# Two matmuls in place of three in the up projection of a two-layer decoder trunk

## The chip, the cores and the metric

The kernel runs on one core of one Trainium2 chip. The metric is the device time of one execution in microseconds (us), taken by the hardware. Engine names: PE is TensorE (PEld its weight loads), DVE is VectorE, ACT is ScalarE, POOL is GpSimd, SP is SyncE, which issues the weight transfers.

## What is computed

The reference is a trunk of two layers on 256 positions of width 1024, all in float32. Each layer has a mixer (attention in three branches, gated) and then a two-step feed-forward part, which is what the change touches:

```
x = x + y @ w_out
hm = rms_norm(x, g_mlp)
x = x + jnp.square(jax.nn.relu(hm @ w_up)) @ w_down      # w_up 1024 x 4096, w_down 4096 x 1024
```

## The kernel before

**Precision.** PE multiplies operands rounded to a shorter float (type fp32r). To come near float32 each operand is split in two: `hi`, the rounded value, which ACT writes, and `lo`, the rest, which DVE writes. A product then takes three matmuls, hi by hi, hi by lo, lo by hi, all accumulated in one PSUM bank; `mm3` (L144 to L147) issues them. In its calls the first argument pair is the stationary operand (loaded by a weight load) and the second the moving one.

**Groups.** The whole program is a list of groups, in an order written by hand. A unit is one weight transfer of up to 1 MB into one of three `raw` buffers; a group is a part of a unit, whose weights are split to `whi` and `wlo` (five buffers each) by `split_to`, L136 on ACT and L137 on DVE. The loop at the end of the kernel goes through the groups: it emits the matmuls of group j, then the split of group j+3 (`LOOK = 3`), then the transfers of the units after it, then deferred work, then the evacuation of group j. Every engine runs its own instructions strictly in that order.

**The feed-forward part of a layer.** `feat_half(l, "mlp", n)` transposes the residual stream and writes the activations as `mlpT`: two tile pairs (`ahi`, `alo`), each 128 x 4 x 256, with four of the eight slices of the 1024 features; they begin 4 elements behind a boundary of 64 elements (`FWD`), where those of the mixer begin on it. `up_first` computes the first 512 columns of the up projection, four tiles of 128 columns with one PSUM bank each; `up_unit(c)` computes 256 columns, two tiles that share one bank, in the second of its two groups. For each tile and each of the eight feature slices `mm3` runs with 128 x 128 weights as stationary operand and 256 positions as moving one. `up_evac(c, p)` (L687 to L701) evacuates them: ACT takes the relu out of PSUM (L695, or L693 twice where the tiles have a bank each), ACT squares it into `uh` (L698), DVE squares it into `sq` (L699), and DVE subtracts `uh` from it to give `ul` (L700). `down_unit(c, n)` multiplies `uh`, `ul` of two `up_unit`s by 512 columns of `w_down`, 24 matmuls of 512 columns, into four banks that stay open through the layer (`dacc`). The order is `up_first`, `up_unit(2)`, and then for c from 0 to 7: `down_unit(c, 0)`, `up_unit(2c+3)`, `down_unit(c, 1)`, `up_unit(2c+4)`. In layer 0 the key and value projections of the memory for layer 1 stand behind `down_unit(4, 1)`.

**PSUM.** `ps()` takes the bank that has been free longest out of eight, `pf()` gives it back.

Of the kernel before, what the change touches and what calls it, by code (L numbers as in the profile page):

```python
# [40 lines left out]
def hybrid_kernel(ctx, tc, x, mem, memT, gains, g_final, rope, masks, w_in, w_pa, w_pb, w_pm,  # L41
# [20 lines left out]
    def sb(shape, dt, tag, bufs, shift=None):  # L62

        n = int(np.prod(shape[1:]))
        if n * (2 if dt == BF16 else 4) % (4 * LINE):
            return small.tile(shape, dt, tag=tag, name=tag, bufs=bufs)
        if shift is None:  # L70
            return pool.tile(shape, dt, tag=tag, name=tag, bufs=bufs)
        t = pool.tile([shape[0], n + LINE], dt, tag=tag, name=tag, bufs=bufs)[:, shift:shift + n]
        return t if len(shape) == 2 else t.rearrange("p (a b) -> p a b", a=shape[1])

    LINE, FWD = 64, 4
    BACK = LINE - FWD
# [65 lines left out]
    def mm3(o, lh, ll, rh, rl, start, stop):  # L144
        nc.tensor.matmul(o, lhsT=lh, rhs=rh, start=start, stop=False)  # L145
        nc.tensor.matmul(o, lhsT=lh, rhs=rl, start=False, stop=False)  # L146
        nc.tensor.matmul(o, lhsT=ll, rhs=rh, start=False, stop=stop)  # L147


# [85 lines left out]
    def qk_unit(l, col, kind, key0, rope_it, act, wsrc, ntile, rows_key):  # L235
        st = {}

        def emit(first, last, ks):
            def f(hi, lo):
# [3 lines left out]
                for i in range(ntile):  # L243
                    for c, k in enumerate(ks):
                        ah, al = tiles[k // 4]
                        mm3(st["p"][i][:, :S], hi[:, c, i * P:(i + 1) * P],
                            lo[:, c, i * P:(i + 1) * P], ah[:, k % 4, :], al[:, k % 4, :],
                            k == 0, k == KT - 1)
# [30 lines left out]
    def v_unit(l, col, n, act, wsrc, key, rows):  # L279
# [3 lines left out]
        def emit(first, last, ks):  # L283
            def f(hi, lo):
# [3 lines left out]
                for t in range(2):  # L288
                    for c, k in enumerate(ks):
                        ah, al = tiles[k // 4]  # L290
                        tt = slice(t * P, (t + 1) * P)
# [180 lines left out]
    def layer(l):  # L472
# [10 lines left out]
        for n in range(2):  # L483
            for br in range(3):
# [3 lines left out]
                def emit(first, last, ks, br=br, n=n, b=b):  # L488
                    def f(hi, lo):
                        if first:  # L490
                            b["p"] = [ps() for _ in range(2)]
                        for t in range(2):
                            tt = slice(t * P, (t + 1) * P)
                            for c, k in enumerate(ks):
                                ah, al = st["hT"][k // 4]
                                mm3(b["p"][t], ah[:, k % 4, tt], al[:, k % 4, tt], hi[:, c, :],
                                    lo[:, c, :], k == 0, k == KT - 1)
# [72 lines left out]
        for n in range(2):  # L570
# [59 lines left out]
            def y_transpose(n=n):  # L630
                for t in range(2):
# [4 lines left out]
                    if t == 0:  # L636
                        st["yT", n] = (sb([P, 4, S], F32R, "ahi", 2, 0),
                                       sb([P, 4, S], F32R, "alo", 2, 0))
                    hi, lo = st["yT", n]
                    tt = slice(t * P, (t + 1) * P)  # L640
# [7 lines left out]
        for half in range(2):  # L648
            for n in range(2):
                def emit(first, last, ks, half=half, n=n):  # L650
                    def f(hi, lo):
# [3 lines left out]
                        for t in range(2):  # L655
                            tt = slice(t * P, (t + 1) * P)
                            for c, k in enumerate(ks):
                                ah, al = st["yT", k // 4]
                                mm3(acc[t, n], ah[:, k % 4, tt], al[:, k % 4, tt], hi[:, c, :],
# [26 lines left out]
        def up_evac(c, p):  # L686
# [3 lines left out]
            ul = sb([P, 2, S], F32R, "qk", 11, 0)  # L690
            if len(p) == 2:
                for i in range(2):
                    nc.scalar.activation(tt[:, i, :], p[i][:, :S], AF.Relu)  # L693
            else:
                nc.scalar.activation(tt.rearrange("p a t -> p (a t)"), p[0], AF.Relu)  # L695
            for t in p:
                pf(t)
            nc.scalar.activation(uh, tt, AF.Square)  # L698
            nc.vector.tensor_tensor(sq, tt, tt, op=ALU.mult)  # L699
            nc.vector.tensor_sub(ul, sq, f32(uh))  # L700
            us[c] = (uh, ul)  # L701

        def up_first():
            b = {}

            def emit(ks):
                def f(hi, lo):
                    if ks[0] == 0:
                        b["p"] = [ps() for _ in range(4)]
                    for i in range(4):  # L710
                        for cc, k in enumerate(ks):
                            ah, al = st["mlpT"][k // 4]
                            mm3(b["p"][i][:, :S], hi[:, cc, i * P:(i + 1) * P],
                                lo[:, cc, i * P:(i + 1) * P], ah[:, k % 4, :], al[:, k % 4, :],
                                k == 0, k == KT - 1)
                    if ks[-1] == KT - 1:
# [10 lines left out]
        def up_unit(c):  # L727
            b = {}

            def emit(last):  # L730
                def f(hi, lo):
                    if not last:
                        b["w"] = (hi, lo)
                        return None
                    p = ps()
                    for i in range(2):
                        for (wh, wl), k0 in ((b["w"], 0), ((hi, lo), 4)):
                            ah, al = st["mlpT"][k0 // 4]
                            for cc in range(4):
                                mm3(p[:, i * S:(i + 1) * S], wh[:, cc, i * P:(i + 1) * P],  # L740
                                    wl[:, cc, i * P:(i + 1) * P], ah[:, cc, :], al[:, cc, :],
                                    k0 + cc == 0, k0 + cc == KT - 1)
                    return lambda: up_evac(c, [p])
                return f
# [114 lines left out]
    def feat_half(l, what, n):  # L859
# [4 lines left out]
        if n == 0:  # L864
            L[ll][dst] = []
        shift = FWD if what == "mlp" else 0
        hi = sb([P, 4, S], F32R, "ahi", 2, shift)
        lo = sb([P, 4, S], F32R, "alo", 2, shift)
        L[ll][dst].append((hi, lo))
        for kp in range(2):  # L870
# [121 lines left out]
    def w_load(k, c):  # L992
# [20 lines left out]

    L[0]["hT"] = [(sb([P, 4, S], F32R, "ahi", 2, 0), sb([P, 4, S], F32R, "alo", 2, 0))
                  for _ in range(2)]

# [8 lines left out]
    def first_operand(k):  # L1025
        hi, lo = L[0]["hT"][k // 4]
        p = first_ps[k // 2]
# [127 lines left out]
```

## Time and profile before

| | before |
|---|---|
| device time, median of 3 runs | 776.96 us (775.22 to 777.06) |
| the profiled execution: device time | 775.68 us |
| its span, first to last instruction | 773.9 us |
| mean granted TensorE clock | 0.998 |
| PE busy | 759.4 us, 4749 matmuls |
| DVE busy | 545.1 us |
| ACT busy | 463.4 us |
| read from HBM | 137.52 MB |

The busy time of PE counts the whole life of a matmul, and matmuls overlap: a stream of them is read by the distance from one start to the next. Idle time of an engine costs nothing unless PE waits for it.

### The profile page before, as it was taken

What the parts mean: (1) busy time and instruction counts of PE and PEld (TensorE: products, weight loads), DVE (VectorE), ACT (ScalarE), POOL (GpSimd) and SP (SyncE); (2) the same over time, 40 slices, a digit from 0 to 9 for tenths busy, and PEclk for the clock granted to TensorE, in tenths of its full rate; (3) what the DMA queues carried; (4) which work ended last, traced back from release to release, by engine and by line L of the source; (5) the groups of instructions that cost most, each with busy time, mean ns of one, the idle gap of its engine ahead of it and who ended that gap; (6) DMA issues with size and microseconds to landing.
All of it is one profiled execution on the core that took longest, in us unless ns stands there. A gap on an engine that the chain in (4) does not pass through costs nothing.

```text
span 773.9 us, 12157 instructions
## 1 busy us (share of the span) xinstructions
PE 759.4 (98%) x4749; PEld 687.7 (89%) x4749; DVE 545.1 (70%) x905; ACT 463.4 (60%) x784; POOL 73.9 (10%) x79
## 2 busy tenths in 40 slices
PE   8999999999999999999999999999999999999996
PEld 6998899888899989998989899988889998999895
DVE  4899999759674655666468899987787656545554
ACT  5687878883573454565455877868546535444542
POOL 1333030003000000000004221200110000000000
PEclk9999999999999999999999999999999999999999
DMA  8847454544656547645536454443565564566431
GB/s 282 278 146 242 153 166 137 186 136 164 218 164 218 194 154 251 217 164 176 192 123 215 157 186 151 164 163 136 191 207 164 174 217 165 165 216 230 161 127 54
DMA packets 92201, 139.35 MB, mean 180 GB/s; under 512 B 2928, under 2 KB 53104, under 8 KB 92144
## 3 DMA queue, kind: packets, MB, share of 16 engines
q1 hardware_dynamic: 92000, 138.55, 54.2%
q8 instruction: 37, 0.61, 0.3%
q14 instruction: 20, 0.16, 0.1%
q10 hardware_dynamic: 144, 0.02, 0.0%
HBM read 137.52 MB, written 1.05 MB: 179 GB/s over the span
## 4 chain that ended last, share of the span: by engine, by line
PE 57%; issue 30%; DVE 7%; ACT 4%; POOL 2%; DMA 1%; POOLq 0%; ACTq 0%; DVEq 0%
PE ps_b L146 17%; PE ps_b L145 17%; PE ps_b L147 17%; DVE wlo L137 2%; PE ps_b L412 1%; ACT whi L136 1%; DVE qk L206 1%; PE ps_b L439 1%; POOL rs L225 1%; POOL rc L226 1%; PE ps_b L332 1%; PE ps_b L331 1%; PE ps_b L438 1%; DMA raw<-in_w_mkv 1%; PE ps_b L1041 0%
## 5 line engine op out<-in xcount | busy, mean ns | idle before, releaser
L137 DVE TENSOR_TENSOR wlo<-raw,whi 128x1024 fp32r<-128x1024 f32 (+2 forms) x266 | 307.8, 1180 | 62.9 <-ACT whi L136 58.5
L136 ACT ACTIVATE whi<-raw 128x1024 fp32r<-128x1024 f32 (+2 forms) x266 | 260.4, 1008 | 54.7 <-PE ps_b L147 41.2
L145 PE MATMUL ps_b<-ahi,whi 128*128 128x256 f32 x736 | 207.2, 282 | 0.0
L147 PE MATMUL ps_b<-ahi,wlo 128*128 128x256 f32 x736 | 206.1, 280 | 0.0
L146 PE MATMUL ps_b<-alo,whi 128*128 128x256 f32 x736 | 206.0, 280 | 0.0
L146 PEld LDWEIGHTS ps_b<-alo,whi 128*128 128x128 f32 x736 | 138.1, 188 | 1.2
L145 PEld LDWEIGHTS ps_b<-ahi,whi 128*128 128x128 f32 x736 | 138.1, 188 | 1.2
L147 PEld LDWEIGHTS ps_b<-ahi,wlo 128*128 128x128 f32 x736 | 138.0, 188 | 0.0
L145 PE MATMUL ps_b<-whi,ahi 128*128 128x512 f32 (+1 forms) x320 | 125.1, 391 | 1.8 <-ACT whi L136 1.8
L146 PE MATMUL ps_b<-wlo,ahi 128*128 128x512 f32 (+1 forms) x320 | 121.5, 380 | 0.5 <-DVE wlo L137 0.5
L147 PE MATMUL ps_b<-whi,alo 128*128 128x512 f32 (+1 forms) x320 | 121.5, 380 | 0.0
L147 PE MATMUL ps_b<-whi,qk 128*128 128x512 f32 x256 | 100.2, 391 | 0.0
L146 PE MATMUL ps_b<-wlo,qk 128*128 128x512 f32 x256 | 100.1, 391 | 0.0
L145 PE MATMUL ps_b<-whi,qk 128*128 128x512 f32 x256 | 99.8, 390 | 0.0
L699 DVE TENSOR_TENSOR P<-P 128x512 f32<-128x512 f32 x32 | 22.1, 692 | 106.7 <-ACT P L695 103.7
L695 ACT ACTIVATE P<-ps_b 128x512 f32<-128x512 f32 x28 | 16.7, 597 | 121.9 <-PE ps_b L147 121.9
L145 PEld LDWEIGHTS ps_b<-whi,ahi 128*128 128x128 f32 x320 | 60.2, 188 | 11.1 <-ACT whi L136 2.6
L147 PEld LDWEIGHTS ps_b<-whi,alo 128*128 128x128 f32 x320 | 60.1, 188 | 10.3
L146 PEld LDWEIGHTS ps_b<-wlo,ahi 128*128 128x128 f32 x320 | 60.3, 188 | 9.6 <-DVE wlo L137 1.1
L147 PEld LDWEIGHTS ps_b<-whi,qk 128*128 128x128 f32 x256 | 48.0, 188 | 10.2
L146 PEld LDWEIGHTS ps_b<-wlo,qk 128*128 128x128 f32 x256 | 48.1, 188 | 9.4
L145 PEld LDWEIGHTS ps_b<-whi,qk 128*128 128x128 f32 x256 | 48.1, 188 | 9.3
(146 smaller groups left out, 882.4 us busy)
## 6 DMA issues: line engine op xcount, KB each, us to landing
raw<-in_w_up SPq DMA_DIRECT2D x32, 1024.0 KB, 5.7
raw<-in_w_down SPq DMA_DIRECT2D x32, 1024.0 KB, 5.0
raw<-in_w_in SPq DMA_DIRECT2D x24, 1024.0 KB, 5.1
raw<-in_w_in SPq DMA_DIRECT2D x24, 768.0 KB, 4.6
raw<-in_w_out SPq DMA_DIRECT2D x8, 1024.0 KB, 5.0
raw<-in_w_mkv SPq DMA_DIRECT2D x4, 1024.0 KB, 5.3
raw<-in_w_pm SPq DMA_DIRECT2D x4, 512.0 KB, 3.3
raw<-in_w_pb SPq DMA_DIRECT2D x4, 512.0 KB, 3.5
```

Source lines behind the costliest of these rows:

```text
L136: nc.scalar.activation(hi, src, AF.Copy)
L137: nc.vector.tensor_sub(lo, src, f32(hi))
L145: nc.tensor.matmul(o, lhsT=lh, rhs=rh, start=start, stop=False)
L146: nc.tensor.matmul(o, lhsT=lh, rhs=rl, start=False, stop=False)
L147: nc.tensor.matmul(o, lhsT=ll, rhs=rh, start=False, stop=stop)
L206: nc.vector.tensor_sub(q[b, j, :], qf[a, :], f32(q[a, j, :]))
L225: nc.gpsimd.tensor_tensor(sh, sh, sinr, op=ALU.mult)
L226: nc.gpsimd.tensor_tensor(c, c, sh, op=ALU.add)
L331: nc.tensor.matmul(p[:, o:o + n], lhsT=qt, rhs=ka[:, j, :n], start=True, stop=False)
L332: nc.tensor.matmul(p[:, o:o + n], lhsT=qt, rhs=kb[:, j, :n], start=False, stop=True)
L695: nc.scalar.activation(tt.rearrange("p a t -> p (a t)"), p[0], AF.Relu)
L699: nc.vector.tensor_tensor(sq, tt, tt, op=ALU.mult)
```

## The change

The activations become one tile `ax` of 128 x 2 x 4 x 256 with both halves in it, `operand(shift)`, so that one access pattern can take the hi and the lo half of a feature slice, 2 x 256 columns 1024 elements apart. It replaces the pairs `ahi`, `alo` everywhere, also in the mixer, which still reads them as two halves. For `mlpT` it begins 8 elements behind the boundary (`HALF`), not 4. In the up projection `mm2` takes the place of `mm3`: one matmul of 512 columns, the hi weights by both halves, and one of 256, the lo weights by the hi half, into the first 256 columns. The product of the hi weights with the lo half stands in the last 256 columns of the bank, and `up_evac` adds it. Each tile of `up_unit` now has a bank of its own.

```diff
+    def mm2(o, lh, ll, rr, start, stop):
+        nc.tensor.matmul(o, lhsT=lh, rhs=rr, start=start, stop=False)
+        nc.tensor.matmul(o[:, :S], lhsT=ll, rhs=rr[:, 0, :], start=False, stop=stop)
+
+    def operand(shift=0):
+        t = sb([P, 2, 4, S], F32R, "ax", 2, shift)
+        return t[:, 0], t[:, 1], t
...
-            if len(p) == 2:
-                for i in range(2):
-                    nc.scalar.activation(tt[:, i, :], p[i][:, :S], AF.Relu)
-            else:
-                nc.scalar.activation(tt.rearrange("p a t -> p (a t)"), p[0], AF.Relu)
-            for t in p:
-                pf(t)
-            nc.scalar.activation(uh, tt, AF.Square)
-            nc.vector.tensor_tensor(sq, tt, tt, op=ALU.mult)
+            for i in range(2):
+                nc.scalar.activation(tt[:, i, :], p[i][:, S:], AF.Copy)
+            for i in range(2):
+                nc.vector.tensor_tensor(tt[:, i, :], p[i][:, :S], tt[:, i, :], op=ALU.add)
+                pf(p[i])
+            nc.vector.scalar_tensor_tensor(sq, tt, 0.0, tt, op0=ALU.max, op1=ALU.mult)
+            nc.scalar.activation(uh, sq, AF.Copy)
             nc.vector.tensor_sub(ul, sq, f32(uh))
...
-                            ah, al = st["mlpT"][k // 4]
-                            mm3(b["p"][i][:, :S], hi[:, cc, i * P:(i + 1) * P],
-                                lo[:, cc, i * P:(i + 1) * P], ah[:, k % 4, :], al[:, k % 4, :],
-                                k == 0, k == KT - 1)
+                            mm2(b["p"][i], hi[:, cc, i * P:(i + 1) * P],
+                                lo[:, cc, i * P:(i + 1) * P],
+                                st["mlpT"][k // 4][2][:, :, k % 4, :], k == 0, k == KT - 1)
...
-                    p = ps()
+                    p = [ps() for _ in range(2)]
                     for i in range(2):
                         for (wh, wl), k0 in ((b["w"], 0), ((hi, lo), 4)):
-                            ah, al = st["mlpT"][k0 // 4]
                             for cc in range(4):
-                                mm3(p[:, i * S:(i + 1) * S], wh[:, cc, i * P:(i + 1) * P],
-                                    wl[:, cc, i * P:(i + 1) * P], ah[:, cc, :], al[:, cc, :],
+                                mm2(p[i], wh[:, cc, i * P:(i + 1) * P],
+                                    wl[:, cc, i * P:(i + 1) * P],
+                                    st["mlpT"][k0 // 4][2][:, :, cc, :],
                                     k0 + cc == 0, k0 + cc == KT - 1)
-                    return lambda: up_evac(c, [p])
+                    return lambda: up_evac(c, p)
...
-        shift = FWD if what == "mlp" else 0
-        hi = sb([P, 4, S], F32R, "ahi", 2, shift)
-        lo = sb([P, 4, S], F32R, "alo", 2, shift)
-        L[ll][dst].append((hi, lo))
+        hi, lo, both = operand(HALF if what == "mlp" else 0)
+        L[ll][dst].append((hi, lo, both))
```

## Rows read from the trace of the kernel before

**Rows 1.** The profile page: busy time by engine, and granted clock by slice.

```profile
PE 759.4 (98%) x4749; PEld 687.7 (89%) x4749; DVE 545.1 (70%) x905; ACT 463.4 (60%) x784; POOL 73.9 (10%) x79
PEclk9999999999999999999999999999999999999999
```

**Rows 2.** Busy time by stretch, steady feed-forward parts of layers 0 and 1.

```profile
core 0: us, PE busy (x) PEld busy (x) DVE busy (x) ACT busy (x) POOL busy (x), PEclk, DMA share, GB/s
239.15:384.50 145.35, 145.35 (x963) 133.53 (x962) 84.38 (x92) 73.38 (x95) 0.00 (x0) 1.00 0.59 194
615.00:750.00 135.00, 135.00 (x873) 123.26 (x872) 73.17 (x72) 61.65 (x72) 0.00 (x0) 1.00 0.56 186
```

**Rows 3.** Timeline of PE: starts (first column) at the edges of an up unit.

```profile
233.26 0.28 PE L145 MATMUL ps_b<-ahi,whi 128*128 128x256 f32 x1
233.38 0.28 PE L146 MATMUL ps_b<-alo,whi 128*128 128x256 f32 x1
233.50 0.28 PE L147 MATMUL ps_b<-ahi,wlo 128*128 128x256 f32 x1
...
238.95 0.39 PE L145 MATMUL ps_b<-whi,qk 128*128 128x512 f32 x1
239.19 0.40 PE L146 MATMUL ps_b<-wlo,qk 128*128 128x512 f32 x1
```

**Rows 4.** Timeline of PE: the last 60 matmuls of 512 columns.

```profile
752.92 0.39 PE L147 MATMUL ps_b<-whi,qk 128*128 128x512 f32 x1
...
766.30 0.39 PE L146 MATMUL ps_b<-wlo,qk 128*128 128x512 f32 x1
```

**Rows 5.** Timeline of PE: 256 columns elsewhere, memory keys, then queries and keys.

```profile
341.34 0.28 PE L146 MATMUL ps_b<-wlo,gate 128*128 128x256 f32 x1
...
343.50 0.28 PE L147 MATMUL ps_b<-whi,gate 128*128 128x256 f32 x1
...
413.14 0.28 PE L146 MATMUL ps_b<-alo,whi 128*128 128x256 f32 x1
...
417.93 0.28 PE L147 MATMUL ps_b<-ahi,wlo 128*128 128x256 f32 x1
```

**Rows 6.** Timeline of ACT, DVE and SP around one evacuation.

```profile
261.51 0.60 ACT L695 ACTIVATE P<-ps_b 128x512 f32<-128x512 f32 x1 [4.64 <-PE ps_b L147]
262.14 0.64 ACT L698 ACTIVATE qk<-P 128x512 fp32r<-128x512 f32 x1
262.68 2.94 ACT L136 ACTIVATE whi<-raw 128x1024 fp32r<-128x1024 f32 x3
...
262.14 0.69 DVE L699 TENSOR_TENSOR P<-P 128x512 f32<-128x512 f32 x1 [4.01 <-ACT P L695]
262.94 0.69 DVE L700 TENSOR_TENSOR qk<-P,qk 128x512 fp32r<-128x512 f32 x1
263.76 3.49 DVE L137 TENSOR_TENSOR wlo<-raw,whi 128x1024 fp32r<-128x1024 f32 x3
...
265.01 0.37 SPq L121 DMA_DIRECT2D raw<-in_w_down  x1
```

**Rows 7.** Timeline of PE: starts of the next two units behind that evacuation.

```profile
261.31 0.39 PE L145 MATMUL ps_b<-whi,qk 128*128 128x512 f32 x1
...
266.80 0.28 PE L145 MATMUL ps_b<-ahi,whi 128*128 128x256 f32 x1
...
268.22 0.28 PE L145 MATMUL ps_b<-ahi,whi 128*128 128x256 f32 x1
```

**Rows 8.** Groups of instructions by form: the nearest kin of the new evacuation.

```profile
L223 DVE TENSOR_TENSOR rc<-cosr,ps_b 128x256 f32<-128x256 f32 x24 | 10.0, 415 | 0.1
L851 DVE SCALAR_TENSOR_TENSOR x<-ps_b,r,x 128x512 f32<-128x512 f32 x7 | 5.2, 749 | 7.7 <-PE ps_b L147 7.7
L693 ACT ACTIVATE P<-ps_b 128x256 f32<-128x256 f32 x8 | 3.0, 379 | 5.7 <-PE ps_b L147 5.5
```

**Rows 9.** Who waited for whom: total us, times, longest.

```profile
ACT P L695 <- PE ps_b L147: 121.9, 28, 4.6
```

**Rows 10.** The profile page, transfers: KB each, median us from issue to landing.

```profile
raw<-in_w_down SPq DMA_DIRECT2D x32, 1024.0 KB, 5.0
```

More of the change, by code (lines that the diff above doesn't have):

```diff
@@ L72, in sb @@
         t = pool.tile([shape[0], n + LINE], dt, tag=tag, name=tag, bufs=bufs)[:, shift:shift + n]
-        return t if len(shape) == 2 else t.rearrange("p (a b) -> p a b", a=shape[1])
-    LINE, FWD = 64, 4
+        names = "abc"[:len(shape) - 1]
+        return t.rearrange(f"p ({' '.join(names)}) -> p {' '.join(names)}",
+                           **dict(zip(names[1:], shape[2:])))
+    LINE, FWD, HALF = 64, 4, 8
     BACK = LINE - FWD
@@ L244, in f @@
                     for c, k in enumerate(ks):
-                        ah, al = tiles[k // 4]
+                        ah, al = tiles[k // 4][:2]
                         mm3(st["p"][i][:, :S], hi[:, c, i * P:(i + 1) * P],
@@ L289, in f @@
                     for c, k in enumerate(ks):
-                        ah, al = tiles[k // 4]
+                        ah, al = tiles[k // 4][:2]
                         tt = slice(t * P, (t + 1) * P)
@@ L494, in f @@
                             for c, k in enumerate(ks):
-                                ah, al = st["hT"][k // 4]
+                                ah, al, _ = st["hT"][k // 4]
                                 mm3(b["p"][t], ah[:, k % 4, tt], al[:, k % 4, tt], hi[:, c, :],
@@ L636, in y_transpose @@
                     if t == 0:
-                        st["yT", n] = (sb([P, 4, S], F32R, "ahi", 2, 0),
-                                       sb([P, 4, S], F32R, "alo", 2, 0))
-                    hi, lo = st["yT", n]
+                        st["yT", n] = operand()
+                    hi, lo, _ = st["yT", n]
                     tt = slice(t * P, (t + 1) * P)
@@ L657, in f @@
                             for c, k in enumerate(ks):
-                                ah, al = st["yT", k // 4]
+                                ah, al, _ = st["yT", k // 4]
                                 mm3(acc[t, n], ah[:, k % 4, tt], al[:, k % 4, tt], hi[:, c, :],
@@ L1011, in hybrid_kernel @@
     nc.sync.dma_start(mask, masks)
-    L[0]["hT"] = [(sb([P, 4, S], F32R, "ahi", 2, 0), sb([P, 4, S], F32R, "alo", 2, 0))
-                  for _ in range(2)]
+    L[0]["hT"] = [operand() for _ in range(2)]
     first_ps = {}
@@ L1025, in first_operand @@
     def first_operand(k):
-        hi, lo = L[0]["hT"][k // 4]
+        hi, lo, _ = L[0]["hT"][k // 4]
         p = first_ps[k // 2]
```

## The prediction

> **What bounds the kernel now.** I read the page first. PE is busy 98% of the span, and every slice shows a granted clock of nine tenths or more [rows 1]; the stretch views give 1.00, the 2.4 GHz level [rows 2]. So neither a cold clock nor a slow stage is to be mended. The same stretch view, over the steady feed-forward parts of both layers, is the one that matters, because all that is changed lies there: PE is busy for the whole of 145.35 and 135.00 us, while DVE works 58 and 54% of them, ACT 50 and 46%, and the DMA engines 59 and 56%. A busy PE is no proof of a full one, so I went on to the timeline of PE, and read distances from start to start. One up unit runs from 233.26 to 238.95 [rows 3]: 48 matmuls of 256 columns in 5.69 us, 118.5 ns each, with no gap inside. The last 60 matmuls of 512 columns start 13.38 us apart, first to last [rows 4]: 59 steps of 226.8 ns. Twice 118.5 is 237.0, so 512 columns in two matmuls cost 10.2 ns more than in one. This is all that the change can win: it streams just as many columns as before, 768 for each tile and slice. The waits say why nothing else wins: in 28 evacuations ACT sat idle 121.9 us in all until PE was done [rows 9], so ACT and DVE wait for PE and not PE for them.
>
> **PE: the sum.** `up_first` has 4 tiles by 8 slices, 32 sets of three matmuls; each of the 14 `up_unit`s has 2 by 8, 16 sets. That is 256 sets a layer and 512 in all. A set costs 3 x 118.5 = 355.5 ns now. It becomes one matmul of 512 columns and one of 256. At the paces of rows 3 and 4 these are 226.8 + 118.5 = 345.3 ns, 10.2 ns less; 512 times that is 5.2 us. One weight load in three goes too, 512 of 4749, but loads run beside matmuls and I give nothing for it on its own.
>
> Both paces are borrowed. For the 256 columns the trace has a faster stretch, the memory keys: 19 steps in 2.16 us, 113.7 ns; and a slower one, queries and keys of layer 1: 40 steps in 4.79 us, 119.8 ns [rows 5]. Same width, same three-way pattern, other operands and other offsets in their tiles; so up to 6 ns hang on where operands lie, and the change moves `mlpT` from 4 elements behind the boundary to 8. For the 512 columns the faster end is 226.8 (no stretch is lower); the slower end is the first step of a down unit, 238.95 to 239.19, 240 ns as rounded [rows 3]. A set thus lies between 226.8 + 113.7 = 340.5 and 240 + 119.8 = 359.8 ns, which is 7.7 us won to 2.2 us lost. I take 345.3, since the up unit's own pace is the nearest row for 256 columns, and the long even run for 512 is nearer to an unbroken stream than the first step behind another unit.
>
> The trace shows no moving operand in two pieces: every one is a single run of 256 or 512 columns. Below, a break between pieces costs nothing (the columns are streamed either way, so I exclude a gain); above, as much as the boundary of two matmuls, 10.2 ns, which would eat the win. I take nothing, as the end that adds no instruction, and keep the other as a rival.
>
> A rule of the Trainium skill speaks against the change: "TensorE: Matmul & The Clock Gate", section "Wait — 56ns, not 53.3ns?", puts the fixed cost of a matmul in a warm stream at about 2.5 ns over its columns. As an estimate by that page, 512 matmuls fewer would give only 1.3 us. The trace does not agree: rows 3 and 4 differ by 10.2 ns a matmul; but part of that may belong to something other than the number of matmuls, and then the rule's small figure would be nearer.
>
> **The evacuation: added work, hidden.** Now ACT takes 0.60 us (L695) and 0.64 (L698), DVE 0.69 twice (L699, L700) [rows 6]. After: ACT copies two halves of 256 columns at 0.379 each, like L693, and makes `uh` as before, 1.40 in all against 1.24; DVE adds two halves at 0.415, like L223, takes relu and square in one instruction of 512, at least 0.69 like L699 and at most 0.749 like L851, and subtracts in 0.69: 2.21 to 2.27 against 1.38 [rows 6, 8]. Over 32 evacuations that is 5 us of ACT and 28 us of DVE; both have some 40% of these stretches free [rows 2], so the busy time alone costs nothing.
>
> What counts is the chain, since each engine is in order. `uh` now waits for DVE, and ACT's next weight split waits behind it. Today: the unit ends at 261.31 [rows 7], the relu starts at 261.51, the next `wlo` split at 263.76 and is done at 265.01, where SP issues the transfer that waited for its buffer [rows 6]. After: the first tile is complete half a unit earlier, so its copy and sum are done. The second tile's copy runs 261.5 to 261.9, its sum to 262.3, relu and square to 263.1, `uh` to 263.75; then `whi` (2.94 / 3, about 1.0) to 264.75 and `wlo` (3.49 / 3, about 1.2) to 266.0, 1.0 us later than now. This split belongs to the second group of the next up unit. That unit starts at 266.80 and first needs it after 12 matmuls, at 268.22 [rows 7]; with faster units 0.2 earlier, 268.0. So the slack falls from 3.2 to 2.0 us and PE does not wait. Behind `up_first` two evacuations stand in a row, some 2 us more work in the chain; the same count leaves about 1.2 us there. Cover gone would show at once: every microsecond that the split is late beyond this would stop PE in each of 28 up units.
>
> The queue behind: SP's transfer is issued 1.0 us later, at 266.0. At 5.0 us to landing [rows 10] its data are there at 271.0. They are split behind the next up unit's evacuation; two periods lie between 238.95 and 261.31 [rows 3, 7], so one is 11.18 us and that is from 263.76 + 11.2 = 274.9 on. Hidden by 4 us. Two banks for each `up_unit` in place of one: four are held by `dacc`, four are left, so two units alternate, and a bank is used again a whole unit of `down` later. The tile `ax` joins two tiles that were always taken and released together; in the mixer nothing is issued more or less. There the offsets of operands beyond the boundary of 64 change; I take no change, with 6 ns on some 670 matmuls of 256 columns of queries and keys, 4 us, as the bound in both directions [rows 5].
>
> **Sum.** 5.2 us off. The profiled execution took 775.68 us (span 773.9, 1.8 around it), so 770.5. The median of the runs shown is 776.96, which gives 771.8. The two differ by more than I can place; I put the time between them, 771.1.
>
> **Rivals.**
> - *A larger win.* The lo weights are now loaded behind 512 columns and not 256, and the hi ones of the next set behind 256 as now. If the excess of 118.5 over 113.7 comes from loads that barely fit behind 256 columns, the set falls to 340.5 ns: 7.7 us, 768.6 us. For it: 113.7 exists. Against: the memory keys have the same loads behind the same columns and run at it already, so it may be only where operands lie. Chance 0.18.
> - *Nothing to speak of.* The break in the moving operand costs what a boundary of two matmuls costs, 10.2 ns, or only a small part of 10.2 belongs to the number of matmuls, as the page has it: 0 to 1.3 us, 775.0 to 776.3. For it: no row with a broken operand. Against: both plain paces are even over dozens of steps. Chance 0.12.
> - *Slower.* The two-piece operand is read worse than a boundary: 512 columns at the 240 ns of the first step behind another unit, plus a break of 10.2, with 256 at 119.8: 370.0 ns a set, 14.5 more, 7.4 us, 783.7. It decides from 345.3 + 10.2 on: each ns beyond costs 0.5 us. Against it: the 240 stands only in the first steps of a unit. Chance 0.06. The late split is part of no sum: it needs 2.0 us more than I count.
>
> **How the numbers follow.** The forecast has the remaining chance, 0.64: 3.5 to 6.5 us won, 769.8 to 772.8. A measurement of this kernel tells about 0.3%, 2.3 us, from no change. Faster by more: the forecast and the larger win, 0.82. Within: 0.12. Slower: 0.06. The range takes in the larger win with a microsecond from the mixer's offsets and the edge of nothing, 767.0 to 775.2, and leaves the rest of the two others out.
>
> **What would show it.** In the new profile: 4237 matmuls; no idle PE inside the feed-forward parts; a set in the timeline at about 345 ns, an up unit at 5.52 us against 5.69; down units unchanged; `wlo` about 1 us later behind each evacuation; DVE some 28 us busier. Wrong would be: a matmul of 512 columns in `mm2` above 237 ns; starts of the up unit's 13th matmul waiting for `wlo`; or another pace in the queries and keys of the mixer, which would move the total by something that the up projection has no part in.

## The result and the profile after

| | before | after |
|---|---|---|
| device time, median of 6 runs each | 776.38 us (775.00 to 777.06) | 770.21 us (770.00 to 771.88) |
| ratio, 95% interval | | 0.9928 (0.9916 to 0.9939) |
| profiled execution: device time, span | 775.68, 773.9 us | 771.88, 770.1 us |
| mean granted clock | 0.998 | 0.999 |
| feed-forward parts of both layers, from the start of `up_first` to the last start of a matmul in the last unit | 370.6 us | 365.8 us |
| a set of one tile and slice, median over 26 up units | 356.0 ns | 347.9 ns |
| a step of 512 columns, median over the down units | 228.5 ns | 227.2 ns |

The kernel is faster by 0.72% by the ratio, which is 5.6 us of 776.38 (4.7 to 6.5 by the interval); the two medians lie 6.2 us apart. The forecast was 771.1 us. A set's time is the length of an up unit, from its first start to the first start of the next unit, over 16; a step's time is that of a down unit over 24. A set consisted of three matmuls before and consists of two now.

The page of the profile after: busy time, share of the span, number of instructions ([rows 1] before).

```profile
PE 755.7 (98%) x4237; PEld 663.6 (86%) x4237; DVE 569.1 (74%) x969; ACT 466.8 (61%) x812; POOL 73.9 (10%) x79
```

There are 512 matmuls and 512 weight loads fewer, and DVE is 24.0 us busier. The same stretches of the feed-forward parts as [rows 2], a little earlier by the time won:

```profile
core 0: us, PE busy (x) PEld busy (x) DVE busy (x) ACT busy (x) POOL busy (x), PEclk, DMA share, GB/s
237.88:382.20 144.32, 144.32 (x776) 125.02 (x776) 93.62 (x117) 74.77 (x106) 0.00 (x0) 1.00 0.62 203
612.00:746.00 134.00, 134.00 (x685) 114.60 (x684) 83.42 (x98) 63.93 (x85) 0.00 (x0) 1.00 0.59 197
```

PE is still busy without a break at a clock of 1.00, so what was won was won in the pace of PE, not in a wait. DVE now works 65 and 62% of these stretches. The timeline of PE over one up unit of after ([rows 3] before; first column the start):

```profile
267.05 0.40 PE L154 MATMUL ps_b<-ax,whi 128*128 128x512 f32 x1
267.28 0.28 PE L155 MATMUL ps_b<-ax,wlo 128*128 128x256 f32 x1
267.40 0.40 PE L154 MATMUL ps_b<-ax,whi 128*128 128x512 f32 x1
...
268.11 0.39 PE L154 MATMUL ps_b<-ax,whi 128*128 128x512 f32 x1
268.33 0.28 PE L155 MATMUL ps_b<-ax,wlo 128*128 128x256 f32 x1
268.45 0.39 PE L154 MATMUL ps_b<-ax,whi 128*128 128x512 f32 x1
268.68 0.28 PE L155 MATMUL ps_b<-ax,wlo 128*128 128x256 f32 x1
...
272.61 0.39 PE L148 MATMUL ps_b<-whi,qk 128*128 128x512 f32 x1
```

From 267.05 to 272.61 are 5.56 us for 16 sets, 347.5 ns each (5.69 us before). The first three sets take 353 ns each (1.06 us to 268.11), the other thirteen 346 ns. Now ACT, DVE and SP of after behind the unit that ends at 261.59 ([rows 6] before):

```profile
261.79 0.39 ACT L703 ACTIVATE P<-ps_b 128x256 f32<-128x256 f32 x1 [2.39 <-PE ps_b L155]
263.40 0.63 ACT L708 ACTIVATE qk<-P 128x512 fp32r<-128x512 f32 x1 [1.22 <-DVE P L707]
263.93 1.05 ACT L139 ACTIVATE whi<-raw 128x1024 fp32r<-128x1024 f32 x1
...
262.21 0.42 DVE L705 TENSOR_TENSOR P<-ps_b,P 128x256 f32<-128x256 f32 x1 [2.35 <-ACT P L703]
262.67 0.69 DVE L707 SCALAR_TENSOR_TENSOR P<-P 128x512 f32<-128x512 f32 x1
264.06 0.69 DVE L709 TENSOR_TENSOR qk<-P,qk 128x512 fp32r<-128x512 f32 x1 [0.70 <-ACT qk L708]
265.01 1.23 DVE L140 TENSOR_TENSOR wlo<-raw,whi 128x1024 fp32r<-128x1024 f32 x1 [0.26 <-ACT whi L139]
...
266.27 0.37 SPq L124 DMA_DIRECT2D raw<-in_w_down  x1
```

`wlo` is done at 266.24, 4.65 us behind the end of the unit just evacuated (3.70 before). Of the next up unit the fifth set is the first to use it, at 268.68: 2.4 us to spare. The tightest place is the first down unit behind `up_first` and the up unit after it: DVE and PE of after there.

```profile
233.21 1.23 DVE L140 TENSOR_TENSOR wlo<-raw,whi 128x1024 fp32r<-128x1024 f32 x1 [0.26 <-ACT whi L139]
...
233.99 0.40 PE L154 MATMUL ps_b<-ax,whi 128*128 128x512 f32 x1
...
235.62 0.28 PE L155 MATMUL ps_b<-ax,wlo 128*128 128x256 f32 x1
```

`wlo` is done at 234.44, and the fifth set takes it at 235.62: 1.2 us to spare. The groups of after by form, costliest forms of the up projection and the added DVE work (busy us, mean ns | idle before):

```profile
L154 PE MATMUL ps_b<-ax,whi 128*128 128x512 f32 x512 | 179.5, 391 | 0.0
L155 PE MATMUL ps_b<-ax,wlo 128*128 128x256 f32 x512 | 144.3, 282 | 0.0
...
L705 DVE TENSOR_TENSOR P<-ps_b,P 128x256 f32<-128x256 f32 x64 | 26.7, 423 | 76.1 <-ACT P L703 76.1
...
L707 DVE SCALAR_TENSOR_TENSOR P<-P 128x512 f32<-128x512 f32 x32 | 22.1, 692 | 1.1
```

The 0.0 behind both matmuls says that PE never stood idle ahead of one in the up projection.

The profiled execution of after is the slowest of its six. Its feed-forward parts are 4.8 us shorter than before, but its first mixer took 209.62 us against 208.45, although nothing was issued there that was not issued before. The place is the start. After:

```profile
8.09 0.63 PE L150 MATMUL ps_b<-whi,ax 128*128 128x512 f32 x1
8.52 0.63 PE L148 MATMUL ps_b<-whi,ax 128*128 128x512 f32 x1
8.94 0.63 PE L149 MATMUL ps_b<-wlo,ax 128*128 128x512 f32 x1
```

These stand 0.43 us apart; before, matmuls of the same place and width stood 0.23 us apart (8.06, 8.30, 8.53 in its timeline). In the execution of the ninth experiment below, with the same code there, they stand at 0.23 too, and its device time was 770.12. The same slow start stands in two more of the profiles, those of the experiments that put the count back at offset 8 and that close the break. So it belongs to single executions, and not to the change. Why it differs was not settled.

### The profile page after: what moved, and what is told of

Same layout as the page of the kernel before. It is cut to its first block, busy times and chain, and to the rows that moved or that the text cites. A ratio compares the mean times of both kernels' runs of the same rounds, so it can differ in the third digit from the quotient of the medians.

```text
span 770.1 us, 11176 instructions
## 1 busy us (share of the span) xinstructions
PE 755.7 (98%) x4237; PEld 663.6 (86%) x4237; DVE 569.1 (74%) x969; ACT 466.8 (61%) x812; POOL 73.9 (10%) x79
## 4 chain that ended last, share of the span: by engine, by line
PE 57%; issue 29%; DVE 7%; ACT 4%; POOL 2%; DMA 1%; POOLq 0%; ACTq 0%; DVEq 0%
PE ps_b L148 13%; PE ps_b L149 13%; PE ps_b L150 13%; PE ps_b L154 8%; PE ps_b L155 4%; DVE wlo L140 2%; PE ps_b L424 1%; ACT whi L139 1%; DVE qk L218 1%; PE ps_b L451 1%; POOL rs L237 1%; PE ps_b L344 1%; POOL rc L238 1%; PE ps_b L343 1%; PE ps_b L450 1%
## 5 line engine op out<-in xcount | busy, mean ns | idle before, releaser
L154 PE MATMUL ps_b<-ax,whi 128*128 128x512 f32 x512 | 179.5, 391 | 0.0
L155 PE MATMUL ps_b<-ax,wlo 128*128 128x256 f32 x512 | 144.3, 282 | 0.0
L148 PE MATMUL ps_b<-whi,ax 128*128 128x512 f32 (+1 forms) x320 | 125.6, 393 | 1.8 <-ACT whi L139 1.8
L149 PE MATMUL ps_b<-wlo,ax 128*128 128x512 f32 (+1 forms) x320 | 122.1, 381 | 0.2 <-DVE wlo L140 0.2
L150 PE MATMUL ps_b<-whi,ax 128*128 128x512 f32 (+1 forms) x320 | 122.0, 381 | 0.0
L154 PEld LDWEIGHTS ps_b<-ax,whi 128*128 128x128 f32 x512 | 96.1, 188 | 20.6
L155 PEld LDWEIGHTS ps_b<-ax,wlo 128*128 128x128 f32 x512 | 96.7, 189 | 1.1
L705 DVE TENSOR_TENSOR P<-ps_b,P 128x256 f32<-128x256 f32 x64 | 26.7, 423 | 76.1 <-ACT P L703 76.1
L148 PEld LDWEIGHTS ps_b<-whi,ax 128*128 128x128 f32 x320 | 60.4, 189 | 11.1 <-ACT whi L139 2.6
L150 PEld LDWEIGHTS ps_b<-whi,ax 128*128 128x128 f32 x320 | 60.3, 189 | 10.4
L149 PEld LDWEIGHTS ps_b<-wlo,ax 128*128 128x128 f32 x320 | 60.5, 189 | 9.6 <-DVE wlo L140 1.0
L148 PE MATMUL ps_b<-ax,whi 128*128 128x256 f32 x224 | 63.6, 284 | 0.0
L149 PE MATMUL ps_b<-ax,whi 128*128 128x256 f32 x224 | 62.7, 280 | 0.0
L150 PE MATMUL ps_b<-ax,wlo 128*128 128x256 f32 x224 | 62.7, 280 | 0.0
```

The costliest lines, as they stand in the source:

```text
L154: nc.tensor.matmul(o, lhsT=lh, rhs=rr, start=start, stop=False)
L155: nc.tensor.matmul(o[:, :S], lhsT=ll, rhs=rr[:, 0, :], start=False, stop=stop)
L705: nc.vector.tensor_tensor(tt[:, i, :], p[i][:, :S], tt[:, i, :], op=ALU.add)
```

## The experiments

Two things changed at once for PE: the number of matmuls, and the offset of `mlpT` behind its boundary, from 4 elements to 8, which the prediction put at nothing. Most of the experiments take these apart. Ratios are against the kernel before on the same chip.

**The tile and its offset alone.** The tile `ax` stays, with its 8 elements, but the up projection goes back to three matmuls, one bank and the old evacuation.

```diff
...
-                                mm2(p[i], wh[:, cc, i * P:(i + 1) * P],
...
+                                ah, al = st["mlpT"][k0 // 4][:2]
+                                mm3(p[:, i * S:(i + 1) * S], wh[:, cc, i * P:(i + 1) * P],
...
```

> The joint tile ax and its shift of 8 alone: up projection by three matmuls of 256 again, the old evacuation, one bank for two tiles. Theory 'number of matmuls': three steps of 118.5 ns, 355.5 a set, total like before, ratio to before 0.999 to 1.001. Rival 'where operands lie': the new tile itself makes part of the win, steps of 116 ns or less in the up units, ratio 0.997 or below. Down units: 228.5 ns a step if the old evacuation made them slow, 227.2 if the layout did.

Measured: ratio 0.9953 (0.9940 to 0.9965), 771.80 us. A set takes 350.2 ns with three matmuls, the feed-forward parts 367.3 us. So 3.3 of the 4.8 us come with no matmul saved. The theory that the number of matmuls alone does it is wrong.

**The offset alone, in the kernel before.** One number.

```diff
-        shift = FWD if what == "mlp" else 0
+        shift = 2 * FWD if what == "mlp" else 0
```

> The kernel before with one number changed: the up projection's activations begin 8 elements behind the boundary, not 4; separate tiles, three matmuls of 256, the old evacuation. Theory 'the offset makes the steps shorter': a set of 350 ns as with the joint tile, down units at 227.7 ns a step, ratio to before 0.9955. Rival 'the joint tile does': a set of 356 ns, ratio 1.000.

Measured: ratio 0.9948 (0.9933 to 0.9962), 771.98 us; set 350.1 ns, feed-forward 367.3 us, as in the experiment above. The joint tile does nothing by itself; the offset does it. One up unit in its timeline, first start and first start of the next unit:

```profile
254.73 0.28 PE L145 MATMUL ps_b<-ahi,whi 128*128 128x256 f32 x1
...
260.33 0.39 PE L145 MATMUL ps_b<-whi,qk 128*128 128x512 f32 x1
```

48 matmuls in 5.60 us, 116.7 ns each, where [rows 3] gave 118.5.

**The count alone.** The changed kernel with `mlpT` back at 4 elements.

```diff
-        hi, lo, both = operand(HALF if what == "mlp" else 0)
+        hi, lo, both = operand(FWD if what == "mlp" else 0)
```

> The changed kernel with the up projection's activations 4 elements behind the boundary, as before, in place of 8. 'Number of matmuls': same set of 347.7 ns, ratio to before 0.993. Rival 'where operands lie': the set is slower by 4 ns or more, 2 us, ratio 0.9955 or above.

Measured: ratio 0.9949 (0.9929 to 0.9968), 771.03 us; set 347.5 ns, feed-forward 366.5 us. That is 0.7 us more than after, and it lies in the down units (228.6 ns a step against 227.2), not in the sets.

```profile
254.66 0.39 PE L154 MATMUL ps_b<-ax,whi 128*128 128x512 f32 x1
...
260.22 0.40 PE L148 MATMUL ps_b<-whi,qk 128*128 128x512 f32 x1
```

5.56 us, the same as in the changed kernel. With the three runs above, a set in ns:

| | offset 4 | offset 8 |
|---|---|---|
| three matmuls | 356.0 (before) | 350.1 |
| two matmuls | 347.5 | 347.9 (after) |

At offset 4 the matmul saved is worth 8.5 ns, near the 10.2 of the prediction. At offset 8 it is worth 2.2 (3.0 if the whole difference of the feed-forward parts, 367.3 against 365.8 us, is laid on 512 matmuls). Either edit brings most of the gain, and the two don't add.

**One unit of the kernel before does not fit the table.** The 356.0 is a median: 25 of the 26 units stand between 355.9 and 356.1 ns a set, and one at 340.1. It is the up unit behind the memory projections in layer 0, with the same three matmuls and the same offset of 4. The timeline of PE before: where the memory keys begin, where the memory values begin, and this unit from its first start to the next unit's.

```profile
333.88 0.28 PE L145 MATMUL ps_b<-gate,whi 128*128 128x256 f32 x1
...
339.50 0.28 PE L145 MATMUL ps_b<-whi,gate 128*128 128x256 f32 x1
...
344.97 0.28 PE L145 MATMUL ps_b<-ahi,whi 128*128 128x256 f32 x1
...
350.41 0.40 PE L145 MATMUL ps_b<-whi,qk 128*128 128x512 f32 x1
```

48 matmuls in 5.44 us are 113.3 ns each, the pace that the memory values had reached just ahead of it, and half of the 226.7 ns at which 512 columns settle (below). At that pace three matmuls of 256 columns cost as much as one of 512 and one of 256, 340.0 ns, and no up unit of the changed kernel is as fast. So offset and number of matmuls do not fix the pace by themselves. What else does is not isolated by this unit: the DMA share was 0.22 in this unit and 1.00 in most others, but the last up unit (744.69 to 750.38), with 0.45, ran at 356.0, and at offset 8 the unit at this place takes 350.4 (three matmuls) and 347.5 (two).

**The count, put back at offset 8.** In the changed kernel the wide matmul is split in two for seven of the eight slices (the one that starts a bank stays whole): 448 matmuls more, with bank and evacuation as changed.

```diff
-        nc.tensor.matmul(o, lhsT=lh, rhs=rr, start=start, stop=False)
+        if start:
+            nc.tensor.matmul(o, lhsT=lh, rhs=rr, start=start, stop=False)
+        else:
+            nc.tensor.matmul(o[:, :S], lhsT=lh, rhs=rr[:, 0, :], start=False, stop=False)
+            nc.tensor.matmul(o[:, S:], lhsT=lh, rhs=rr[:, 1, :], start=False, stop=False)
```

> The changed kernel with the hi weights' matmul of 512 columns split into its two halves of 256 for seven of eight feature slices, 448 matmuls more, the same numbers and the same evacuation. 'Number of matmuls': a set of 3 x 118.5 = 355.5 ns against 347.7, 448 x 7.8 = 3.5 us more than the change, ratio to before 0.997. Rival 'evacuation and banks': nothing comes back, ratio 0.993. Rival 'only 2.5 ns a matmul': 1.1 us, ratio 0.994. Down units stay at 227.2 ns a step if the new evacuation made them faster.

Measured: ratio 0.9978 (0.9965 to 0.9991), 773.60 us; set 350.3 ns, 2.4 more than after. That is 2.4 x 512 / 448 = 2.7 ns for each matmul added. The feed-forward parts take 368.5 us, 2.7 more: 1.2 in the sets, and some 1.5 in the down units, whose steps went from 227.2 to 229.2 ns though nothing in them was edited. Laid on the 448 matmuls as a whole, 2.7 us are 6.0 ns each. So the set speaks for the small price, and the total (0.9978 against an expected 0.997) for the larger one.

**A matmul's boundary in the down units.** There weights and activations both begin on the boundary. Each matmul of 512 columns is split in two of 256, except for the first three of each bank: 744 more.

```diff
-                    mm3(dacc[t, n], uh[:, k % 2, tt], ul[:, k % 2, tt], hi[:, cc, :],
-                        lo[:, cc, :], c == 0 and k == 0, c == 7 and k == 3)
+                    if c == 0 and k == 0:
+                        mm3(dacc[t, n], uh[:, k % 2, tt], ul[:, k % 2, tt], hi[:, cc, :],
+                            lo[:, cc, :], True, False)
+                        continue
+                    for h in range(2):
+                        cs = slice(h * S, (h + 1) * S)
+                        mm3(dacc[t, n][:, cs], uh[:, k % 2, tt], ul[:, k % 2, tt], hi[:, cc, cs],
+                            lo[:, cc, cs], False, h == 1 and c == 7 and k == 3)
```

> The changed kernel with the matmuls of 512 columns in the down projection split into two of 256, 744 more, the same numbers. Here weights and activations both lie on the boundary. If a matmul beyond costs 8 to 10 ns whatever the operands: down units of 24 sets' worth 5.65 us or more against 5.45, 6 to 7.6 us in all over the change. If it costs 2.5 ns: 1.9 us. If two narrow steps are as fast as one wide: 226.8 ns for the two, nothing.

Measured, one run: 779.81 us; feed-forward parts 375.1 us, 9.3 more than after, 12.5 ns for each matmul added, more than any of the three cases expected. One down unit:

```profile
249.75 0.28 PE L148 MATMUL ps_b<-whi,qk 128*128 128x256 f32 x1
...
255.50 0.40 PE L154 MATMUL ps_b<-ax,whi 128*128 128x512 f32 x1
```

48 matmuls in 5.75 us, 119.8 ns each. So a boundary between matmuls costs 12.5 ns here and 2.2 to 2.7 in the up projection of the changed kernel, with the same width and the same clock.

This run shows more. The memory projections were not edited, and they changed pace. Its memory values:

```profile
340.30 0.28 PE L148 MATMUL ps_b<-whi,gate 128*128 128x256 f32 x1
...
346.00 0.39 PE L154 MATMUL ps_b<-ax,whi 128*128 128x512 f32 x1
```

48 matmuls take 5.70 us, 118.8 ns each, where the kernel before (339.50 to 344.97) and the changed kernel (338.79 to 344.26) both took 5.47 us, 113.9 ns, with the same operands at the same offsets. In all three stretches the clock is 1.00 and ACT and DVE work 3.1 us each; the DMA share is 0.63 here, 0.63 before and 0.84 after. What differs from the changed kernel is the down units ahead. So the pace of a stream also depends on what ran before it.

**The offset at 16.** The kernel before with four times `FWD`.

```diff
-        shift = FWD if what == "mlp" else 0
+        shift = 4 * FWD if what == "mlp" else 0
```

> The kernel before with the up projection's activations 16 elements behind the boundary, not 4: three matmuls of 256, nothing else changed. The steps of 256 columns so far: 120 ns at a distance of 0 (down units split in two), 118.7 at 4, 116.7 at 8. If that goes on in a line: 113 ns at 16, 339 ns a set, which would beat the changed kernel's 347.9: ratio to before 0.988. If 8 is the end of it: 350 ns a set, ratio 0.995. If it comes back: 356 ns, ratio 1.000.

Measured: ratio 0.9988 (0.9978 to 0.9998), 774.39 us; set 353.6 ns, feed-forward 369.4 us. It lies between offset 4 (356.0) and offset 8 (350.1): further is not better, and 8 is the best of the three that ran with three matmuls.

**The same distance from the other side.** In the changed kernel `mlpT` on the boundary and the up weights 4 elements ahead of one (`BACK`), as in the queries and keys.

```diff
-                     [emit([k0, k0 + 1]), emit([k0 + 2, k0 + 3])])
+                     [emit([k0, k0 + 1]), emit([k0 + 2, k0 + 3])], BACK)
...
-            unit([(wu[:, :, c * 256:(c + 1) * 256], 8)], 8, 256, [4, 4], [emit(False), emit(True)])
+            unit([(wu[:, :, c * 256:(c + 1) * 256], 8)], 8, 256, [4, 4], [emit(False), emit(True)], BACK)
...
-        hi, lo, both = operand(HALF if what == "mlp" else 0)
+        hi, lo, both = operand(0)
```

> The changed kernel with the up projection's weights 60 elements behind the boundary and its activations on it, the offsets at which the memory keys run their matmuls of 256 columns in 113 to 114 ns. If the pair of offsets decides: 226.8 + 113.4 = 340 ns a set against 347.9, 4 us less than the change, ratio to before 0.988. If only the distance of the two offsets does (4, as in the run with shift 4): 225.3 + 122, 347.5 ns a set, ratio 0.993 to 0.995.

Measured: ratio 0.9967 (0.9952 to 0.9981), 773.43 us; set 352.5 ns, 5.0 more than with weights at 0 and activations at 4. So it is not the distance between the two operands alone. The stretch at 113 to 114 ns that is named here is not that of the memory keys but of the memory values (their rows name the weights first, as the moving operand). The keys, with weights at 60, ran from 333.88 to 339.50, 48 matmuls at 117 ns.

**The lo weights at another offset.** In the changed kernel `wlo` of the up projection begins 4 elements behind the boundary, `whi` on it.

```diff
-            lo = sb([P, 1024], F32R, "wlo", 5, g["shift"])[:, :g["c"] * g["n"]].rearrange(
+            lo = sb([P, 1024], F32R, "wlo", 5, g["lshift"])[:, :g["c"] * g["n"]].rearrange(
...
-            unit([(wu[:, :, c * 256:(c + 1) * 256], 8)], 8, 256, [4, 4], [emit(False), emit(True)])
+            unit([(wu[:, :, c * 256:(c + 1) * 256], 8)], 8, 256, [4, 4], [emit(False), emit(True)], 0, FWD)
```

> The changed kernel with the lo weights of the up projection 4 elements behind the boundary, the hi weights on it and the activations 8 behind it as they are. A step lasts from one matmul to the next, in which the next weights load; at a distance of 4 between activations and weights the wide step was 225.3 ns, at 8 the narrow one 118.4. If each step goes by the distance to the weights that load in it: 225.3 + 118.4 = 343.7 ns a set against 347.9, 2.1 us less than the change, ratio to before 0.990. If the set as a whole is bound near 347: no change, ratio 0.993.

Measured: ratio 0.9931 (0.9912 to 0.9950), 770.63 us; set 346.8 ns, a gain of 1.1 against after, in the median of the units; the total can't be told from that of after. A rule of one price for each distance, which had to give some 3 ns more, falls here too.

**The offset in the mixer.** In the changed kernel the weights of queries and keys begin 8 elements ahead of the boundary and not 4, those of the memory keys as they were.

```diff
-                     BACK)
+                     LINE - HALF)
...
-             [emit(True, False, [0, 1, 2, 3]), emit(False, True, [4, 5, 6, 7])], BACK)
+             [emit(True, False, [0, 1, 2, 3]), emit(False, True, [4, 5, 6, 7])],
+             BACK if key0 == "m" and kind == "k" else LINE - HALF)
```

> The changed kernel with the offset of the weights of the mixer's queries and keys moved from 60 to 56, so that the moving operand lies 8 behind the stationary one there too (without the memory keys). If the distance of the offsets makes the step: 116.7 ns in place of 118.5 or so for 672 matmuls of 256 columns, 1.2 us less than the change, ratio to before 0.991. If it holds in the up projection alone: no change, ratio 0.993.

Measured: ratio 0.9938 (0.9922 to 0.9953), 771.35 us; the mixer of layer 1 took 185.61 us against 185.95, 0.34 won. It has the right sign, but is far less than 6 ns on some 670 matmuls, 4 us, which the prediction kept as its bound for the mixer.

**The break in the moving operand.** In the changed kernel the two halves of a slice lie side by side, so that 512 columns are one run.

```diff
+        if pairs:
+            t = sb([P, 4, 2, S], F32R, "ax", 2, shift)
+            return t[:, :, 0], t[:, :, 1], t.rearrange("p k h t -> p h k t")
...
-        hi, lo, both = operand(HALF if what == "mlp" else 0)
+        hi, lo, both = operand(HALF if what == "mlp" else 0, what == "mlp")
```

> The changed kernel with the two halves of each feature slice beside each other in the up projection's activations, so that the 512 moving columns are one run. If the break between the pieces costs what the wide matmul has over the down units', 1.5 ns: 227.0 in place of 228.5 ns, 0.8 us less than the change, ratio to before 0.992. If the break is free: no change, ratio 0.993, the same 228.5.

Measured: set 347.9 ns and feed-forward parts 365.8 us, both the same as after. The break costs nothing. Ratio 0.9949 (0.9928 to 0.9969), 771.65 us: the interval overlaps that of after, and the difference of the medians does not lie in the feed-forward parts.

**The chain of the evacuation, made later.** In the changed kernel DVE runs three more operations on `sq` that leave it as it is, some 2.15 us in front of `uh`.

```diff
             nc.vector.scalar_tensor_tensor(sq, tt, 0.0, tt, op0=ALU.max, op1=ALU.mult)
+            for _ in range(3):
+                nc.vector.scalar_tensor_tensor(sq, sq, 0.0, sq, op0=ALU.max, op1=ALU.max)
```

> The changed kernel with three more instructions of 0.69 us on VectorE between the relu with square and the activation that waits for it: the evacuation's chain is 2.2 us longer. In the changed kernel the wlo that is needed next is done at 266.25 and first read at 268.67, a slack of 2.4 us. If the slack is as counted: no idle PE in the feed-forward parts, their 365.8 us stay. If it is smaller than 2.2: PE stops in each of some 26 up units by what is missing, 1 us missing gives 26 us.

Measured, one run: 783.42 us; feed-forward parts 378.6 us, 12.8 more than after. In the steady part PE waited nowhere, as 2.4 us to spare had it. But behind `up_first`, where 1.2 us are to spare, three such chains follow one another (two of `up_first`, one of `up_unit(2)`), and PE stood (its timeline, in brackets the idle time ahead):

```profile
230.94 0.51 PE L148 MATMUL ps_b<-whi,qk 128*128 128x512 f32 x1 [0.74 <-ACT whi L139]
232.20 0.51 PE L149 MATMUL ps_b<-wlo,qk 128*128 128x512 f32 x1 [0.76 <-DVE wlo L140]
238.51 0.50 PE L154 MATMUL ps_b<-ax,whi 128*128 128x512 f32 x1 [2.11 <-ACT whi L139]
239.77 0.39 PE L155 MATMUL ps_b<-ax,wlo 128*128 128x256 f32 x1 [0.77 <-DVE wlo L140]
```

4.4 us in all, and the same four waits in layer 1. Layer 0 lost 5.6 us. A part of the rest is that a matmul with a wait on both sides takes its whole 0.5 us, where otherwise the next one starts after 0.23. There the wait had a second price. Stretches of 3 us around it (PE busy, granted clock, DMA share, GB/s):

```profile
core 0: us, PE busy (x), PEclk, DMA share, GB/s
619.00:622.00 3.00, 2.24 (x8) 0.76 0.17 25
622.00:625.00 3.00, 3.00 (x14) 0.67 1.04 393
```

PE stood idle for 0.76 us of the first stretch; behind it the granted clock is 0.67, and matmuls of 512 columns start 0.43 us ahead of the next one (622.14, 622.57), the lower of the two levels, 1.2 GHz, up to 624.03. Layer 1 lost 7.2 us by this edit. In layer 0 the clock stayed at 1.00 behind the same waits.

**Both offsets that helped.** The changed kernel with the lo weights at 4 and the queries and keys at 8: the two edits shown above together.

> The changed kernel with both small gains in it: the mixer's queries and keys with weights at 56, the up projection's lo weights at 4. In the profiles these gave 0.34 us in the mixer of layer 1, as much at best in that of layer 0, and 0.12 us in the feed-forward parts. If they add: feed-forward parts 365.7 us, mixer of layer 1 185.6, in all 0.5 to 0.8 us less than the change, ratio to before 0.992. If the order of weights and offsets works the other way in one of them: the stages of the change, 365.8 and 185.95, ratio 0.993.

Measured: 769.90 us (769.00 to 770.17), ratio 0.9923 (0.9910 to 0.9937); mixer of layer 1 185.63, set 346.8 ns, feed-forward 365.7 us. Each part kept what it gave alone; the total can't be told from the changed kernel's 0.9928.

## Why the prediction came out right, and what in it was wrong

**What bounds the kernel.** Right. PE is busy all the time at a clock of 1.00 before and after, and the gain is pace. By the rows: 512 sets at 8.1 ns less are 4.1 us, 768 steps of down units at 1.3 ns less 1.0 us; together 5.1 us, beside 4.8 read off the feed-forward stages and 5.6 (4.7 to 6.5) by the ratio. (The unit at 340.1 ns a set, which the median leaves out, makes up most of the 0.3.)

**The set.** Forecast 345.3 ns, measured 347.9: 8.1 won where 10.2 were counted, 1.1 us too much over 512. Averaged over the recorded starts of 26 units, the wide step is 229.5 ns and not 226.8, the narrow one 118.4, as counted. The wide term was mis-sized: 226.8 is the pace that a run of one shape settles at. The wide matmuls of the new unit never reach it; they take about 235 ns in the first three sets and 228 in the others.

**"So up to 6 ns hang on where operands lie, and the change moves `mlpT` from 4 elements behind the boundary to 8."** The step was seen and then given nothing, and this is the one that failed. That the total still came out is luck. The offset alone takes a set of three matmuls from 356.0 to 350.1 ns, ratio 0.9948. It did not show in the total because it doesn't add: with two matmuls a set stands at 347.5 and 347.9 at the two offsets. So the price of 10.2 ns for a matmul, read off rows 3 and 4, is no fixed price of a matmul. It is what two matmuls of the up unit ran above the settled pace (twice 118.5 against twice 113.3), and a new offset alone takes 5.9 ns off a set with no matmul saved. In the layout that the change itself makes, a matmul is worth 2.2 to 2.7 ns inside the set. The faster row that the prediction saw, 113.7 ns, was put down to other operands and offsets. It is the memory values, not the keys, and an up unit with the operands and the offset of [rows 3] ran at 113.3 ns behind them.

**The page's rule.** The Trainium skill ("TensorE: Matmul & The Clock Gate", section "Wait — 56ns, not 53.3ns?") has about 2.5 ns for it. At offset 8 the runs agree (2.2 by taking one away, 2.7 by adding one), at offset 4 (8.5) and in the down units (12.5) they do not, and in the unit at 340.1 ns a set three matmuls cost no more than two would at the settled paces. The prediction took rule and rows for rivals. They were prices of two stretches.

**The break** was taken at nothing: right, shown by the halves laid side by side.

**Down units unchanged:** wrong by a little, 227.2 ns a step against 228.5. This made up 1.0 us, nearly what the set fell short, so the sum came out nearer than its terms. The difference lies in the first steps of a down unit: nine are slow before, three after. Before, the unit that starts at 238.95 [rows 3], its tenth matmul and the next unit:

```profile
241.04 0.39 PE L145 MATMUL ps_b<-whi,qk 128*128 128x512 f32 x1
...
244.44 0.28 PE L145 MATMUL ps_b<-ahi,whi 128*128 128x256 f32 x1
```

After, a down unit's first and fourth matmul (the next unit starts at 267.05, shown above):

```profile
261.59 0.39 PE L148 MATMUL ps_b<-whi,qk 128*128 128x512 f32 x1
...
262.29 0.39 PE L148 MATMUL ps_b<-whi,qk 128*128 128x512 f32 x1
```

From there on both run at 226.7 ns a step (before 3.40 us for 15, after 4.76 us to 267.05 for 21). The median of a down step lay between 227.2 and 229.2 ns in all kernels whose down units are alike; why a unit settles sooner behind one up unit than behind another is not shown.

**The evacuation:** right. `wlo` came 0.95 us later against the end of its unit (forecast 1.0), the transfer was issued at 266.27 (266.0), 2.4 us were to spare (2.0), and PE waited nowhere. DVE's added time was 24.0 us, not 28: the new instruction on 512 elements took 692 ns, the lower of its two bounds, and DVE's other work came out 2 us shorter. Behind `up_first` 1.2 us were to spare, as counted, and the late chain showed that this cover is thin: PE stopped there and nowhere else.

**The mixer** was taken as unchanged: 186.08 and 185.95 us in layer 1.

**The rivals.** *A larger win* from lo weights that load behind 512 columns: the set did not fall to 340.5, though 340.1 stood in one unit of the kernel before. *Nothing*: its first cause, the break, is excluded; its second, a small price of a matmul, holds at offset 8, but the offset brought the rest. *Slower*: the wide matmul took 229.5 ns on average, and about 235 only in the first three sets of a unit.

**What stays open.** Why an offset of 4, 8 or 16 elements changes the pace, and how that goes together with what ran before: no rule of distance fits weights at 60 with activations at 0 (352.5 ns), weights at 0 with activations at 4 (347.5), and lo weights at 4 (346.8). That the cause lies in how the two operands are read from memory is only argued. How what ran before acts is open too: with the down units split and nothing else changed, the memory values lost 4.9 ns a matmul, while the up units won 0.8 ns a set (347.1 against 347.9).

## What to carry to other kernels

A price read off one stretch ("a matmul more costs 10 ns") is good for that stretch, with its operands' places and what ran before it. Look at the units that don't fit the median, since here one of 26 showed that the price could be nothing. When an edit also moves an operand by a few elements, run the move alone, since it may be one number that brings 0.5% without the rest. Two edits that each win are not two wins: fill the table of both before adding them. And when a total comes out right, check each term: here two errors of one microsecond cancelled.

## What the runs showed of the hardware that had not been expected

- The start of an operand within 64 elements changes the pace of a stream of TensorE at a granted clock of 1.00. Three matmuls of 256 columns took 356.0, 350.1 and 353.6 ns with the moving operand 4, 8 and 16 elements behind the boundary and the weights on it.
- A stream's pace also depends on what ran before. The same memory values took 113.9 and 118.8 ns a matmul in two kernels that differ in the down units ahead of them, and one up unit of the kernel before took 340.1 ns a set where the 25 others took 356.0.
- Streams settle: steps of 512 columns at 226.7 ns from the tenth of a down unit before and the fourth after, steps of 256 columns at 113.3, exactly half. By these two paces a matmul more would cost nothing.
- The price of splitting a matmul of 512 columns in two was 2.7 ns in one place and 12.5 in another of the same kernel.
- A moving operand in two pieces 1024 elements apart streams as fast as one run: 347.9 ns a set in both.
- After a wait of PE of some 2 us and one of 0.76 in layer 1, the granted clock was 0.67 over 3 us; in layer 0 it stayed at 1.00 after the same waits.
- At the start of an execution four matmuls of 512 columns can stand 0.43 us apart while the granted clock of that stretch is given as 1.00 (8.09 to 9.80 of the profile after); in other executions of the same code they stand at 0.23.
